# A two-layer decoder trunk: one job list for gate and down projections, and where the block sums are made

## The chip, the cores and the metric

The kernel runs on one core of one Trainium2 chip. The metric is the device time of one execution in microseconds (us); of several runs the median is given. A profile of one execution, taken by the hardware profiler, stands beside the times. The engines are called as the profile calls them: PE (TensorE, with PEld for its weight loads), DVE (VectorE), ACT (ScalarE), POOL (GpSimd) and SP (SyncE, which issues loads).

## The reference

One sequence of 512 tokens, 1024 wide, in float32, goes through two layers. The first mixes tokens with a gated short convolution, the second with sliding-window attention (16 heads, 4 key/value heads, window 128, rotary positions, an attention sink). Each layer ends with a SwiGLU feed-forward network of inner width 2816.

```python
def swiglu(h, w_gate_up, w_down):
    g, u = jnp.split(h @ w_gate_up, 2, axis=-1)
    return (jax.nn.silu(g) * u) @ w_down

for l in range(DEPTH):                       # DEPTH = 2
    if l < N_A:                              # layer 0
        mix = short_conv_mixer(rmsnorm(h, a_pre_norm[l]), a_w_in[l], a_conv_w[l], a_w_out[l])
        h = h + rmsnorm(mix, a_post_norm[l])
    else:                                    # layer 1; K and V from the h after layer 0
        ...
        attn = sliding_window_sink_attention(q, k_sh, v_sh, b_sinks[j]) @ b_w_o[j]
        h = h + rmsnorm(attn, b_post_norm[j])
    ff = swiglu(rmsnorm(h, ffn_pre_norm[l]), ffn_w_gate_up[l], ffn_w_down[l])
    h = h + rmsnorm(ff, ffn_post_norm[l])
```

## The kernel before

**Products.** Every matrix product in float32 is made as three products in a faster float32 format (`mm3`, L171). Each weight block of 128 x 1024 numbers (512 KB) is first split: ACT copies it to the high part (`whi`, L167) and DVE subtracts that from the block to get the low part (`wlo`, L168). `split_weights` (L154) does both on a block that `fetch` (L136) has loaded into a raw buffer with a DMA on SP's queue (L141). There are five raw buffers (`N_RAW`) and five pairs of split buffers (`N_W`). A raw buffer comes free, and the next load can start, when the DVE split of its block is done.

**Stages.** Convolution mixer (0 to 139 us of the profiled execution), its output projection and norms (to 185), feed-forward network (FFN) of layer 0 (to 552), K/V and attention (to 696), its output projection (to 720), FFN of layer 1 (to 1080) and the last writes.

**The FFN** (`ffn`, L685). The inner width of 2816 is cut into 22 tiles of 128, f = 0 to 21. The tiles f = 0 to 3 are projected plainly. The other 18 form nine pairs, called q0 to q8 here. A pair's gate and up projections are made by `gate_seven` (L729), a scheme that gets a product of 2 x 2 blocks from seven block products in place of eight, in the order p = 1, 2, 6, 5, 7, 3, 4. Each of the seven is one weight block and 24 matmuls of 256 columns, so a pair has 168. Three of the seven weight blocks are stored blocks (`w_gb`); four are sums of such blocks.

**The sums of gate blocks** (`Sums`, L396) are made in HBM by DMAs that POOL issues (L408): four copies, two additions, one and one more addition, eight DMAs of 512 KB for each pair, 144 in all. `sum_on` (L433) takes one step of each pair in work. They are called in the convolution stage and after the pairs of both FFNs, and the sums of layer 1 are made from layer 0's FFN on. A finished sum is loaded by SP as any other block (`raw<-hsum`).

**The down projection** is made in four rounds over the tiles, `ROUNDS = [(0, 6), (6, 10), (10, 14), (14, 22)]`. Rounds 0 to 2 are called D0, D1 and D2 here; `seven` (L791) does them by the same scheme, with 126, 84 and 84 matmuls of 512 columns. It loads the four blocks, makes four differences of them on DVE in the raw buffers (L820), and splits with three jobs of lead (`SEVEN_LEAD`, L824 on ACT and L825 on DVE). Its products go into `mix` through DVE (L861). The last round is made directly by `first_half` (L546) and `second_half` (L597), with 192 matmuls.

**Order.** For a layer it is f0 to f3, q0, D0, q1, q2, D1, q3, q4, D2, q5, q6, q7, q8, last round. Each of D0 to D2 stands right behind the pair that makes the last of its activations. `pair_sums` (L708) turns a finished pair into the activation blocks of the down projection: small sums and splits on DVE and ACT, all at once behind the pair. In the gate pairs the order of instructions on an engine is left to a scheduler; in `project_first`, `first_half` and `second_half` it is written out by hand (`manual_schedule`).

**Attention.** POOL does part of the rotary step for most query tiles (L975, L976) and the low part of the split (L982, `rlo`), which the score matmuls (L1034) read. Norms use POOL for a power (L271, L293). The letters R and H in the table of steps `ORDER` stand for the rotary step and its split.

Of the kernel before, what the change touches and what calls it, by code (L numbers as in the profile page):

```python
# [10 lines left out]
F32 = mybir.dt.float32  # L11
F32R = mybir.dt.float32r
# [4 lines left out]
P = 128  # L17
D = 1024
# [6 lines left out]
PLAIN = 4  # L25
WARM = 8
LEAD = 2
SEVEN_LEAD = 3
# [10 lines left out]
N_SLOT, N_WIDE, N_RAW, N_W = 43, 14, 5, 5  # L39
# [17 lines left out]
def yoco_kernel(  # L57
# [337 lines left out]

    class Sums:  # L396

        def __init__(self, l, q):  # L400
            self.a = [w_gb[l, q, b] for b in range(4)]
            self.s = [hbm.tile([P, D], F32, name=name("hsum")) for _ in range(4)]
            self.steps = [self.first, self.second, self.third, self.fourth]

        def move(self, dst, src, behind, **kw):
            dst, src = (a.rearrange("(a b) c -> a (b c)", b=2) for a in (dst, src))
            made = tc.keep_in_program_order(
                nc.gpsimd.dma_start(dst, src, max_dma_last_dim=8 * D, **kw))  # L408
            if behind is not None:
                tc.add_manual_dep(made.ins, behind.ins.name, mybir.DependencyInfo(  # L410
                    mybir.DependencyClass.Sync, mybir.DependencyReason.DATA), reason="pace")

        def first(self, behind):
            a11, a12, a21, a22 = self.a
            for s, a in zip(self.s, (a21, a11, a11, a12)):
                self.move(s, a, behind)

        def second(self, behind):
            a11, a12, a21, a22 = self.a
            self.move(self.s[0], a22, behind, accum_op=ALU.add)  # L420
            self.move(self.s[1], a21, behind, accum_op=ALU.add)

        def third(self, behind):
            self.move(self.s[2], self.s[0], behind, accum_op=ALU.add)

        def fourth(self, behind):
            self.move(self.s[3], self.s[2], behind, accum_op=ALU.add)

    sums_of = {(l, q): Sums(l, q) for l in range(2) for q in range((NF - PLAIN) // 2)}
    to_sum = [sums_of[k] for k in sorted(sums_of)]  # L430
    summing = []

    def sum_on(behind=None, more=True):  # L433

        if more and to_sum:
            summing.append(to_sum.pop(0))
        for x in summing:
            x.steps.pop(0)(behind)
        summing[:] = [x for x in summing if x.steps]
# [74 lines left out]
    for f in range(KT):  # L514
# [27 lines left out]
        if 1 <= f < KT - 1:  # L542
            sum_on(more=f % 2)


    def first_half(load, x, n, take, ws1=None):  # L546

        ws = [load(0, j) for j in range(n // 2)]
        raws = [fetch(load(1, j, True)) for j in range(min(2, n // 2))]
        ws1 = []  # L550

        def more():
            if len(ws1) < n // 2:
                ws1.append(split_weights(None, raws.pop(0), True))
                j = len(ws1) + len(raws)
                if j < n // 2:
                    raws.append(fetch(load(1, j, True)))

        with tc.manual_schedule(engines=ALL):
            pss = [bank("pmix") for _ in range(2)]  # L560
            for t in range(2):
                unit(pss[t], t, ws, x, range(n - 2), n)
                more()
# [107 lines left out]
    def load_out(half, j, raw=False):  # L671
        src = w_out[half, j]
        return src if raw else split_weights(src)
# [4 lines left out]

    ws1 = first_half(load_out, ys, KT, take_out)
    ahead = Ahead(first_weights(0))  # L680
# [4 lines left out]
    def ffn(l, before, ahead, gain, gpres, following):  # L685
# [5 lines left out]
        def gate_pair(pg, pu):  # L691
# [6 lines left out]
            self_paced.append(nc.scalar.activation(gr, pg, AF.Silu))  # L698
# [5 lines left out]
            pair_sums(gr)  # L704

        self_paced = []

        def pair_sums(gr):  # L708
# [7 lines left out]
            nc.scalar.activation(h, a11, AF.Copy)  # L716
            nc.vector.tensor_tensor(out=lo, in0=a11, in1=h.bitcast(F32), op=ALU.subtract)
            for o, x, y, op in ((s1, a21, a22, ALU.add), (s2, s1, a11, ALU.subtract),
                                (s3, a11, a21, ALU.subtract), (s4, a12, s2, ALU.subtract)):
                nc.vector.tensor_tensor(out=o, in0=x, in1=y, op=op)  # L720
            t = [(e[:, :256], e[:, 256:])]
            for src in (*sums, gr[:, S:]):
                h, lo = slot("ahi", F32R), slot("alo", F32R)
                nc.scalar.activation(h, src, AF.Copy)
                nc.vector.tensor_tensor(out=lo, in0=src, in1=h.bitcast(F32), op=ALU.subtract)
                t.append((h, lo))
            acts.append(t)

        def gate_seven(q, factors, out):  # L729
# [3 lines left out]
            a, s = sums_of[l, q].a, sums_of[l, q].s  # L733
            srcs = {1: a[0], 2: a[1], 4: a[3], 5: s[0], 6: s[2], 7: s[1], 3: s[3]}
            chain = {1: "X", 6: "X", 7: "X", 4: "X", 5: "Z", 3: "Z", 2: "Y"}
            pools = {"X": ps_mm, "Y": ps_pt, "Z": ps_sc}
            banks = {}
            gr = wide("gr")
            kept = [slot("st") for _ in range(2)]

            def take(p, e):
                x, y, z = (banks[c][e][:, :256] if c in banks else None for c in "XYZ")
                g0, g1 = (gr[:, c : c + 256] for c in (e * S, e * S + 256))
# [9 lines left out]
                elif p == 3:  # L753
                    nc.vector.tensor_tensor(out=g1, in0=z, in1=s, op=ALU.add)  # L754
                    both = gr[:, e * S : (e + 1) * S]
                    self_paced.append(nc.scalar.activation(both, both, AF.Silu))  # L756
# [5 lines left out]
            for p in (1, 2, 6, 5, 7, 3, 4):  # L762
                whi, wlo = split_weights(srcs[p])
                c = chain[p]
                opened = c not in banks
                if opened:
                    banks[c] = [bank("g" + c.lower(), pools[c]) for _ in range(2)]
                for e in range(2):
                    for k in range(4):
                        kk = slice(e * S + k * P, e * S + (k + 1) * P)  # L770
                        mm3(banks[c][e][:, :256], whi[:, kk], wlo[:, kk], *factors[p][k],
                            opened and k == 0, k == 3 and p in (2, 3, 4), skip_group_check=True)
                    take(p, e)
            out(gr)

        def pair_acts(gr):
            for c in (0, S):
# [4 lines left out]
                acts.append((hi, lo))  # L782
# [8 lines left out]
        def seven(kps, acts, first):  # L791
# [3 lines left out]
            raw = {}  # L795
            for b in range(4):
                for c, ks in enumerate(cs):
                    if len(ks) > 1:
                        raw[b, c] = fetch(w_dn[l, kps[ks[0]] : kps[ks[-1]] + 1, b])
                    else:  # L800
                        raw[b, c] = slot("raw")
                        nc.sync.dma_start(raw[b, c], w_dn[l, kps[ks[0]], b])

            factor = {1: (0, None), 5: (0, 1), 6: (0, 2), 3: (2, None), 7: (1, 2), 2: (3, None),
                      4: (0, 3)}
            jobs = [(p, c) for p in (1, 5) for c in range(len(cs))]
            jobs.sort(key=lambda j: j[1])
            jobs += [(p, c) for p in (6, 3, 7, 2, 4) for c in range(len(cs))]
            ready, banks, left_of = {}, {}, {p: len(cs) for p in factor}
# [5 lines left out]
            def prepare(p, c):  # L815
                b, other = factor[p]
                n = S * len(cs[c])
                w = raw[b, c][:, :n]
                if other is not None:
                    nc.vector.tensor_tensor(out=w, in0=raw[other, c][:, :n], in1=w,  # L820
                                            op=ALU.subtract)
                hi = wsp.tile([P, D], F32R, tag="whi", name=name("whi"))
                lo = wsp.tile([P, D], F32R, tag="wlo", name=name("wlo"))
                nc.scalar.activation(hi[:, :n], w, AF.Copy)  # L824
                nc.vector.tensor_tensor(out=lo[:, :n], in0=w, in1=hi[:, :n].bitcast(F32),  # L825
                                        op=ALU.subtract)
                ready[p, c] = hi, lo

            for j in range(min(SEVEN_LEAD, len(jobs))):
                prepare(*jobs[j])  # L830
            for j, (p, c) in enumerate(jobs):
                if j + SEVEN_LEAD < len(jobs):
                    prepare(*jobs[j + SEVEN_LEAD])
                bs = chain[p]
                if bs not in banks:
                    banks[bs] = [bank("p" + bs.lower(), pools[bs]) for _ in range(2)]
                    opened = True
                else:
                    opened = False
                hi, lo = ready.pop((p, c))  # L840
                left_of[p] -= 1
                for n, k in enumerate(cs[c]):
                    kk = slice(n * S, (n + 1) * S)
                    for r in range(2):
# [4 lines left out]
                if left_of[p]:  # L849
                    continue  # L850
# [34 lines left out]
        for i in (0, 2):  # L885
            gate_pair(*pss[i : i + 2])
# [484 lines left out]
```

## Time and profile before

| | before |
|---|---|
| median of 3 runs | 1086.6 us (1084.23 to 1087.57) |
| the profiled execution | 1089.31 us |
| its span in the profile | 1087.5 us |
| mean granted clock of TensorE | 0.984 |
| busy share of DVE, ACT, POOL | 70%, 51%, 16% |
| moved by DMA | 218.87 MB, mean 201 GB/s |

The page gives the busy time of each engine and the granted clock in 40 slices of the span. A row of the chain of waits has a start, a length and what took it. A row of the timeline has a start, a length, the engine, the line, the operation, its tiles, and in brackets the idle time before it with what ended it. Rows of DMA issues give the count, the size of one and the median time from issue to landing. Matmuls overlap, so that the pace of a stage is read from a window and not from the length of one.

### The profile page before, as it was taken

Reading aid. Unit: us, or ns where it says so; the run is one execution under the profiler, and the core shown is the slowest. Engines: PE = TensorE matmul, PEld = TensorE weight load, DVE = VectorE, ACT = ScalarE, POOL = GpSimd, SP = SyncE. Lnnn points to the kernel's source line nnn. Section 1 sums busy time; section 2 is a strip of 40 time slices with the busy share of each in tenths; the row PEclk is TensorE's granted clock in tenths of the full one; section 3 lists DMA queues with packets and bytes.
Section 4 is the critical chain, followed back from the end, with each engine's and each line's share of the span. In section 5 each row is a group of like instructions: output and inputs, shape, how many; then the busy total and the mean of one; then the engine's idle time right before and its main releaser. Section 6 shows DMA issues by size and latency. Waiting matters only on the chain.

```text
span 1087.5 us, 17067 instructions
## 1 busy us (share of the span) xinstructions
PE 1049.0 (96%) x6556; PEld 940.4 (86%) x6556; DVE 766.5 (70%) x1294; ACT 552.8 (51%) x1000; POOL 172.2 (16%) x227
## 2 busy tenths in 40 slices
PE   9999999999998988999999999999999989989997
PEld 7888888998997977999798888898979879789986
DVE  5765555779677776664678998778786866956654
ACT  6322235845552534553475776677466444445531
POOL 0332201012021110121021541020211101200001
PEclk9999999999999899999999999999999999989999
DMA  9577753287779779899712123325797797878621
GB/s 334 176 209 235 215 191 118 78 270 196 250 219 291 243 219 317 297 309 308 255 44 75 40 79 98 108 107 139 232 275 206 229 332 253 228 249 247 204 99 78
DMA packets 58482, 218.87 MB, mean 201 GB/s; under 512 B 7200, under 2 KB 8096, under 8 KB 49184
## 3 DMA queue, kind: packets, MB, share of 16 engines
q1 hardware_dynamic: 46304, 141.62, 36.8%
q0 software_dynamic: 11520, 75.51, 26.9%
q8 instruction: 51, 0.84, 0.3%
q10 hardware_dynamic: 576, 0.66, 0.2%
q14 instruction: 31, 0.25, 0.1%
HBM read 211.46 MB, written 81.79 MB: 270 GB/s over the span
## 4 chain that ended last, share of the span: by engine, by line
PE 67%; DVE 13%; DMA 13%; ACT 4%; issue 3%; POOL 0%; POOLq 0%; DVEq 0%; SPq 0%; ACTq 0%
DMA raw<-in_w_dn_dram 7%; DMA raw<-hsum 5%; PE gx L172 4%; PE gx L173 4%; PE gx L174 4%; PE pmix L172 3%; PE pmix L173 3%; PE pmix L174 3%; PE pgu L172 3%; PE pgu L173 3%; PE pgu L174 3%; DVE wlo L825 3%; PE gz L172 2%; PE gz L173 2%; PE gz L174 2%
## 5 line engine op out<-in xcount | busy, mean ns | idle before, releaser
L168 DVE TENSOR_TENSOR wlo<-raw,whi 128x1024 fp32r<-128x1024 f32 x168 | 215.0, 1282 | 116.2 <-ACT whi L167 116.1
L167 ACT ACTIVATE whi<-raw 128x1024 fp32r<-128x1024 f32 x168 | 176.9, 1056 | 199.1 <-PE gx L173 44.2
L172 PE MATMUL gx<-xt,whi 128*128 128x256 f32 x432 | 126.5, 293 | 17.6 <-ACT st L746 17.1
L173 PE MATMUL gx<-xt,whi 128*128 128x256 f32 x432 | 125.6, 291 | 0.0
L174 PE MATMUL gx<-xt,wlo 128*128 128x256 f32 x432 | 125.6, 291 | 0.0
L172 PEld LDWEIGHTS gx<-xt,whi 128*128 128x128 f32 x432 | 86.4, 200 | 18.7 <-ACT st L746 17.9
L408 POOL DMA_DIRECT2D hsum<-hsum x36 | 28.6, 854 | 435.4 <-ACT gr L756 265.5
L173 PEld LDWEIGHTS gx<-xt,whi 128*128 128x128 f32 x432 | 86.5, 200 | 0.0
L174 PEld LDWEIGHTS gx<-xt,wlo 128*128 128x128 f32 x432 | 86.5, 200 | 0.0
L408 POOL DMA_DIRECT2D hsum<-in_w_gb_dram x108 | 71.8, 1051 | 71.5 <-ACT gr L756 39.4
L824 ACT ACTIVATE whi<-raw 128x1024 fp32r<-128x1024 f32 (+1 forms) x56 | 52.0, 949 | 57.7 <-DVE raw L820 44.8
L825 DVE TENSOR_TENSOR wlo<-raw,whi 128x1024 fp32r<-128x1024 f32 (+1 forms) x56 | 60.2, 1087 | 18.7 <-ACT whi L824 18.6
L172 PE MATMUL pgu<-xlo,whi 128*128 128x256 f32 (+1 forms) x192 | 61.6, 321 | 0.0
L173 PE MATMUL pgu<-xhi,whi 128*128 128x256 f32 (+1 forms) x192 | 61.1, 318 | 0.0
L174 PE MATMUL pgu<-xhi,wlo 128*128 128x256 f32 (+1 forms) x192 | 61.1, 318 | 0.0
L172 PE MATMUL pmix<-wlo,ahi 128*128 128x512 f32 (+1 forms) x136 | 52.3, 385 | 1.9 <-DVE wlo L162 1.9
L173 PE MATMUL pmix<-whi,ahi 128*128 128x512 f32 (+1 forms) x136 | 51.9, 382 | 0.0
L174 PE MATMUL pmix<-whi,alo 128*128 128x512 f32 (+1 forms) x136 | 51.7, 380 | 0.0
L756 ACT ACTIVATE gr<-gr 128x512 f32<-128x512 f32 x36 | 22.5, 625 | 46.7 <-DVE gr L754 46.5
L820 DVE TENSOR_TENSOR raw<-raw,raw 128x1024 f32<-128x1024 f32 (+1 forms) x32 | 34.8, 1088 | 11.4 <-DMA raw<-in_w_dn_dram 10.9
L172 PE MATMUL gz<-xt,whi 128*128 128x256 f32 x144 | 41.1, 286 | 0.0
L173 PE MATMUL gz<-xt,whi 128*128 128x256 f32 x144 | 41.0, 285 | 0.0
(279 smaller groups left out, 3167.3 us busy)
## 6 DMA issues: line engine op xcount, KB each, us to landing
hsum<-in_w_gb_dram POOLq DMA_DIRECT2D x108, 512.0 KB, 11.7
raw<-hsum SPq DMA_DIRECT2D x72, 512.0 KB, 4.7
raw<-in_w_gb_dram SPq DMA_DIRECT2D x54, 512.0 KB, 7.2
raw<-in_w_dn_dram SPq DMA_DIRECT2D x40, 512.0 KB, 9.0
hsum<-hsum POOLq DMA_DIRECT2D x36, 512.0 KB, 6.5
raw<-in_w_in_dram SPq DMA_DIRECT2D x21, 512.0 KB, 7.2
raw<-in_w_gu_dram SPq DMA_DIRECT2D x16, 512.0 KB, 3.6
raw<-in_w_out_dram SPq DMA_DIRECT2D x8, 512.0 KB, 5.9
```

The costliest lines, as they stand in the source:

```text
L167: nc.scalar.activation(hi, raw, AF.Copy)
L168: nc.vector.tensor_tensor(out=lo, in0=raw, in1=hi.bitcast(F32), op=ALU.subtract)
L172: nc.tensor.matmul(out, whi, xlo, start=start, stop=False, **kw)
L173: nc.tensor.matmul(out, whi, xhi, start=False, stop=False, **kw)
L174: nc.tensor.matmul(out, wlo, xhi, start=False, stop=stop, **kw)
L408: nc.gpsimd.dma_start(dst, src, max_dma_last_dim=8 * D, **kw))
L756: self_paced.append(nc.scalar.activation(both, both, AF.Silu))
L820: nc.vector.tensor_tensor(out=w, in0=raw[other, c][:, :n], in1=w, op=ALU.subtract)
L824: nc.scalar.activation(hi[:, :n], w, AF.Copy)
L825: nc.vector.tensor_tensor(out=lo[:, :n], in0=w, in1=hi[:, :n].bitcast(F32), op=ALU.subtract)
```

## The change

**One list.** Gate products, D0 to D2 and the four first-half weight blocks of the last round become `Job`s in one list, run by `in_line` in an order written out by hand. Before job j + 3 is reached it is prepared (`LINE_LEAD`): its block is split by ACT and DVE while job j's products are issued. Raw blocks are fetched in list order. There are seven raw buffers (`N_RAW`) in place of five and four split pairs (`N_W`) in place of five.

**Late down projection.** The order becomes f2, f3, q0, q1, D0, q2, q3, D1, q4, q5, D2, q6, q7, q8, last round: each of D0 to D2 stands one gate pair later. The activation work of a finished pair comes in six parts, one behind each following job, apart from the jobs that are marked `alone`. D0's 14 products of up to two blocks become 11 jobs, as some half-width blocks share a job.

**Sums.** The four differences of D0 to D2 are now made in HBM too, and DVE's subtraction (L820) is gone. Gate pairs q3, q4 and q5 take all four sums from HBM. The other six (`ADDED`) take two from HBM; the blocks for p = 6 and p = 3 are made by `Job.add` on DVE, in place, from blocks that were loaded for other products, so that such a pair loads five blocks. POOL still issues 144 DMAs. `BEGIN` says at which step each set of sums begins: in the convolution stage and in attention without pacing, in attention between the rotary steps, and in the FFN a few behind each job. The sums of layer 1 begin in attention.

**Smaller ones.** Silu of both halves of a pair comes after p = 3. `first_half` takes ready splits and keeps up to three raw blocks loaded. The sign of one half of `mix` is changed, with a scale where it is begun and a subtraction where it is added to. The host lays out the blocks of `w_dn` differently.

```diff
+ADDED = (0, 1, 2, 6, 7, 8)
+BEGIN = {
+    "c0": "g00", "c2": "g01", "c4": "d00", "c6": "g02", "o0": "g03", "o1": "d01", "0f1": "g04",
+    "0f3": "g05", "0p0": "d02", "0p1": "g06", "0s0": "g07", "0p2": "g08",
+    "a0": "g10", "a2": "g11", "a3": "d10", "a5": "g12", "a6": "g13", "a8": "d11", "1f0": "g14",
+    "1f2": "g15", "1p0": "d12", "1p1": "g16", "1s0": "g17", "1p2": "g18",
+}
-SEVEN_LEAD = 3
+LINE_LEAD = 3
-N_SLOT, N_WIDE, N_RAW, N_W = 43, 14, 5, 5
+N_SLOT, N_WIDE, N_RAW, N_W = 43, 14, 7, 4
...
+        def add(self):
+            if self.make:
+                raw = self.raws[0].tile
+                nc.vector.tensor_tensor(out=raw, in0=raw, in1=self.raws[1].tile, op=ALU.add)
+
+        def prepare(self):
...
+            self.begun = nc.scalar.activation(hi[:, :n], raw, AF.Copy)
+            nc.vector.tensor_tensor(out=lo[:, :n], in0=raw, in1=hi[:, :n].bitcast(F32),
+                                    op=ALU.subtract)
...
+    def in_line(jobs, late):
...
+        def prepare(j):
+
+            if 0 <= j < len(jobs):
+                jobs[j].prepare()
+            while n[0] < len(raws) and (n[0] < N_RAW or raws[n[0] - N_RAW].last <= j):
+                raws[n[0]].fetch()
+                n[0] += 1
+            if j + 1 < len(jobs):
+                jobs[j + 1].add()
+
+        for j in range(-1, LINE_LEAD):
+            prepare(j)
+        for j, job in enumerate(jobs):
+            if job.run:
+                job.run(job)
+            prepare(j + LINE_LEAD)
+            if j + LINE_LEAD < len(jobs):
+                issue(1 + len(issues) // 6, jobs[j + LINE_LEAD].begun)
+            if late and not job.alone:
+                late.pop(0)()
+            late += job.then() or [] if job.then else []
...
+            raws = {1: [a11], 2: [a12], 5: [s1], 7: [s3], 4: [a22]}
+            if rest:
+                raws[6], raws[3] = ([r] for r in rest)
+            else:
+                raws[6], raws[3] = [a11, s1], [a12, a11]
...
-                if other is not None:
-                    nc.vector.tensor_tensor(out=w, in0=raw[other, c][:, :n], in1=w,
-                                            op=ALU.subtract)
...
+                order = [[(1, 0)], [(5, 0)], [(1, 1), (5, 1)], [(6, 0)], [(3, 0)],
+                         [(6, 1), (3, 1)], [(7, 0)], [(2, 0)], [(7, 1), (2, 1)], [(4, 0)],
+                         [(4, 1)]]
...
+                    if behind_one:
+                        jobs += behind_one.pop()
...
     with tc.manual_schedule(engines=ALL):
+        sum_on("a0")
         for i in range(KT + 2):
...
+                if op in "RH":
+                    issue(len(issues) // 2 if op == "R" else len(issues))
+            sum_on(f"a{i + 1}")
```

More of the change, by code (lines that the diff above doesn't have):

```diff
@@ L393, in one, with __init__, fetch @@
             self.lo()
-    class Sums:
[L400 to L406, printed above, removed]
+    class Raw:
+        def __init__(self, *srcs):
+            self.srcs = srcs
+            self.widths = [s.shape[0] * S if len(s.shape) == 3 else D for s in srcs]
+            self.n = sum(self.widths)
+        def fetch(self):
+            self.tile, c = wraw.tile([P, D], F32, tag="raw", name=name("raw")), 0
+            for src, n in zip(self.srcs, self.widths):
+                dst = self.tile[:, c : c + n]
+                if len(src.shape) == 3:
+                    src, dst = (src.rearrange("k p c -> p k c"),
+                                dst.rearrange("p (k c) -> p k c", c=S))
+                nc.sync.dma_start(dst, src)
+                c += n
@@ new lines, in yoco_kernel, with __init__, step @@
+    class Sums:
+        def __init__(self, blocks, shape, every=True):
+            self.blocks = blocks
+            n = 4 if every else 2
+            self.sums = [hbm.tile(shape, F32, name=name("hsum")) for _ in range(n)]
+            a, b, c, d = blocks
+            ab, ac, *rest = self.sums
+            self.steps = [[(ab, a, None), (ac, a, None)], [(ab, b, ALU.add), (ac, c, ALU.add)]]
+            if every:
+                abc, abcd = rest
+                self.steps[0] += [(abc, c, None), (abcd, d, None)]
+                self.steps += [[(abc, ab, ALU.add)], [(abcd, abc, ALU.add)]]
+        def step(self):
+            issues.extend(self.steps.pop(0))
@@ L409, in move @@
             if behind is not None:
[L410 to L430, printed above, removed]
+                tc.add_manual_dep(
+                    made.ins, behind.ins.name, mybir.DependencyInfo(
+                        mybir.DependencyClass.Sync, mybir.DependencyReason.DATA),
+                    reason="pace")
@@ L829, in seven, with run, products @@
[L829 to L833, printed above, removed]
+            def run(parts):
+                def products(job):
+                    at = 0
+                    for p, c in parts:
+                        product(p, c, *(w[:, at : at + S * len(cs[c])] for w in job.w))
+                        at += S * len(cs[c])
+                return products
@@ new lines, in ffn, with weights, take_last @@
+            n = f1 - f0
+            def weights(half, j):
+                return w_dn[l, half : 4 - half : 3 - 2 * half, f0 // 2 + j]
+            closing = [Job([Raw(weights(0, j))], None) for j in range(n // 2)]
+            in_line(jobs + closing, late)
+        res = Update(mix, gain, gpres, True)
+        res.load()
+        def take_last(t, half, ps):
+            res.take(t, half, ps)
+            res.scale(t, half)
+        ws1 = first_half(weights, acts[-1], n, take_last, [job.w for job in closing])
```

345 lines of the change are left out of this document (198 added, 147 removed), and 4 rows, old and new, of the table BEGIN.

## The prediction

> **What bounds the kernel now.** I read the page first, then the stages of the two feed-forward networks (FFN) in the windows view, then the chain of waits and the timeline where a stage ran below pace.
>
> ```profile
> span 1087.5 us, 17067 instructions
> PE 1049.0 (96%) x6556; PEld 940.4 (86%) x6556; DVE 766.5 (70%) x1294; ACT 552.8 (51%) x1000; POOL 172.2 (16%) x227
> PEclk9999999999999899999999999999999999989999
> ```
>
> TensorE is busy 96% of the span, so what can be won without removing matmuls is its idle time, and the slices in which its clock fell. The change keeps all matmuls. So I compare each stage with the same work at full pace (columns: us of the window; busy us and instructions of PE, PEld, DVE, ACT, POOL; granted clock; DMA share; GB/s). First the pace:
>
> ```profile
> 41.03:138.95 97.92, 97.92 (x434) 81.08 (x432) 62.41 (x69) 22.15 (x24) 30.64 (x35) 1.00 0.69 205
> 231.62:251.77 20.15, 20.15 (x170) 20.15 (x168) 16.80 (x26) 10.52 (x17) 1.29 (x3) 1.00 0.69 252
> ```
>
> The convolution stage: 432 matmuls of 512 columns in 97.92 us, 0.2267 us each. Pair q0 of layer 0 (168 matmuls of 256 columns): 20.15 us without a gap. Now layer 0's D0, q1-q2, D1, q3-q4, D2, q5-q8 and the last down projection, then the same of layer 1 (without its last):
>
> ```profile
> 251.77:281.42 29.65, 29.14 (x129) 23.51 (x128) 25.24 (x36) 18.05 (x26) 4.69 (x8) 1.00 0.99 276
> 281.42:321.73 40.31, 40.31 (x338) 40.31 (x336) 27.87 (x39) 20.89 (x33) 3.58 (x6) 1.00 0.74 237
> 321.73:343.63 21.90, 20.14 (x87) 15.43 (x85) 21.27 (x34) 10.43 (x13) 6.78 (x10) 1.00 0.86 246
> 343.63:392.66 49.03, 43.54 (x337) 43.13 (x336) 29.99 (x43) 20.47 (x32) 3.59 (x6) 0.93 0.81 255
> 392.66:416.13 23.47, 21.28 (x87) 16.79 (x85) 22.11 (x34) 10.96 (x14) 6.78 (x10) 0.93 0.82 239
> 416.13:502.25 86.12, 82.17 (x674) 81.96 (x672) 51.77 (x71) 42.26 (x64) 12.45 (x20) 0.98 0.96 305
> 502.25:548.62 46.37, 44.43 (x188) 35.79 (x187) 28.82 (x44) 21.93 (x38) 7.09 (x9) 0.96 0.82 264
> 766.75:786.91 20.16, 20.16 (x170) 20.15 (x168) 16.81 (x26) 10.52 (x17) 1.29 (x3) 1.00 0.72 256
> 786.91:816.58 29.67, 29.17 (x129) 23.50 (x128) 25.24 (x36) 18.06 (x26) 4.69 (x8) 1.00 0.98 275
> 816.58:856.90 40.32, 40.32 (x337) 40.32 (x336) 27.48 (x39) 20.78 (x33) 3.60 (x6) 1.00 0.75 237
> 856.90:879.20 22.30, 20.14 (x87) 15.44 (x86) 21.67 (x34) 10.53 (x14) 6.80 (x10) 1.00 0.85 247
> 879.20:925.66 46.46, 42.12 (x337) 41.90 (x336) 30.07 (x43) 20.61 (x32) 3.60 (x6) 0.96 0.84 267
> 925.66:949.10 23.44, 21.25 (x87) 16.75 (x86) 22.12 (x34) 11.07 (x14) 6.80 (x10) 0.93 0.84 240
> 949.10:1036.45 87.35, 83.49 (x674) 83.28 (x672) 55.58 (x77) 45.26 (x67) 2.34 (x3) 0.96 0.75 232
> ```
>
> q0 to q2 are at full pace, and every stage behind D1 is not. D1 and D2 (84 matmuls, 19.04 us) take 21.90 to 23.47 us with DVE busy 94 to 97%: VectorE bounds them. The pairs behind them lose to this:
>
> ```profile
> 337.79 1.23 DVE wlo L825
> 339.04 13.95 DMA raw<-hsum
> 353.08 1.06 ACT whi L167
> 354.46 0.58 PE L172 MATMUL gx<-xt,whi 128*128 128x256 f32 x1 [4.92 <-ACT st L746]
> 349.20:353.80 4.60, 0.34 (x3) 0.14 (x2) 0.55 (x1) 0.72 (x1) 0.00 (x0) 1.00 1.00 317
> 353.80:360.60 6.80, 6.13 (x28) 6.14 (x29) 4.16 (x5) 4.04 (x7) 0.00 (x0) 0.50 0.99 362
> ```
>
> The chain: a late split in D1 frees a raw buffer only at 339.04, the next block sum is fetched then, lands 13.95 us later, and TensorE stands still for 4.3 of 4.6 us. Then the clock is halved for 6.8 us. One such entry costs about 4.3 + 3.4 = 7.7 us.
>
> **Gate pairs.** Layer 0 spends 20.15 + 40.31 + 49.03 + 86.12 = 195.61 us in its nine pairs, 14.26 more than 9 x 20.15 = 181.35; layer 1 spends 20.16 + 40.32 + 46.46 + 87.35 = 194.29, 12.94 more. The change makes one list of split jobs with three jobs of lead, seven raw buffers in place of five, fetched in list order, and puts each down projection one pair behind the activations it needs, so that a pair follows whose blocks were requested before. Counted in the list of jobs, a load is issued at least 22 us of TensorE work before its use, and the longest landing of a sum above took 13.95. Value taken: all 27.2 us; bounds: none of it (below, as a rival) and all of it.
>
> The six pairs that add on DVE cost it 12 extra additions in a layer:
>
> ```profile
> L820 DVE TENSOR_TENSOR raw<-raw,raw 128x1024 f32<-128x1024 f32 (+1 forms) x32 | 34.8, 1088 | 11.4 <-DMA raw<-in_w_dn_dram 10.9
> L168 DVE TENSOR_TENSOR wlo<-raw,whi 128x1024 fp32r<-128x1024 f32 x168 | 215.0, 1282 | 116.2 <-ACT whi L167 116.1
> ```
>
> Two of 1.09 us bring a pair's 16.8 us of DVE (q0's window) to 19.0, of 20.15, so the pair stays under TensorE: cost 0. With that cover gone, each us over 20.15 would be lost six times in a layer. The addition is also a new wait: on the in-order DVE it stands for two loads, the block and its sum, and behind it are the splits of the next jobs and the sums that empty the PSUM banks. If the load of the sum is late, all of DVE is late; that price is in the rival on late loads. SP's queue carries less, not more: 5 loads in place of 7 in these pairs, while the loads of the block sums stay 72 (48 for gates, 24 of 512 KB for downs).
>
> **Down projections D1, D2.** They now load four ready differences: the 32 subtractions of L820 go. Of D1's 21.27 us four full ones (4.35) leave 16.9, below its 19.04 of matmuls; the activation splits, now one behind each job, leave it as well. Excess: 21.90 + 23.47 - 38.08 = 7.29 in layer 0, 22.30 + 23.44 - 38.08 = 7.66 in layer 1. I keep 0.3 us in each of the four for short waits: -13.75; bounds 0 and -14.95.
>
> **D0.** 126 matmuls need 28.57; its excess, 1.08 us in layer 0 and 1.10 in layer 1, is short waits of a product for its split, on a DVE that is busy 85%. Its new list of 11 jobs, half-width ones among them, has about three times as many such close places: +1 us in each layer, between -1.08 (they vanish) and +2.2 (three times 1.08 in place of it).
>
> **Last down projection, layer 0.** 186 matmuls need 42.17 of 46.37 us. The 0.96 DMA share ahead of it, when layer 1's sums were made under q5 to q8, is gone, as these sums now begin in attention. I take -3.5 of 4.2; bounds 0 and -4.2.
>
> **Sums on POOL's queue.** The 144 moves stay 144: fewer for gates, 36 for downs.
>
> ```profile
> hsum<-in_w_gb_dram POOLq DMA_DIRECT2D x108, 512.0 KB, 11.7
> q0 software_dynamic: 11520, 75.51, 26.9%
> q1 hardware_dynamic: 46304, 141.62, 36.8%
> 577.00:696.00 119.00, 118.59 (x781) 99.88 (x780) 105.22 (x321) 82.42 (x243) 33.46 (x24) 1.00 0.21 67
> 626.23 1.70 POOL L982 TENSOR_TENSOR rlo<-ra,rhi 128x512 fp32r<-128x512 f32 x1 [1.54 <-ACT rhi L981]
> 632.35 0.39 PE L1034 MATMUL psc<-rlo,rhi 64*128 64x256 f32 x2
> ```
>
> Some of them now stand on POOL's queue between the rope steps of attention, where TensorE is busy 118.59 of 119 us. A POOL DMA instruction costs it 6.78 / 10 = 0.68 us (D1's window), at most four come ahead of a step, 2.7 us, and `rlo` ends at 627.93, 4.4 us before its scores start. So they are hidden; I put +1 us for the chains with less slack, in attention and at the norms; bounds 0 and +8 (1 us in each of eight steps).
>
> [...]
>
> **Sum.** -27.2 - 13.75 - 3.5 + 2 + 1 = -41.45. The profiled execution took 1089.31 us (span 1087.5 and 1.8 around it): 1047.9. The median of the three runs, 1086.6, is 2.7 below that execution, so 1045.
>
> **The rivals.**
> *Loads land late all the same.* In 210 to 340 us sums and loads together now ask more of the DMA engines. A move takes 26.9% x 1087.5 / 144 = 2.03 us of all 16, a load some 36.8% x 1087.5 / 270 = 1.48. About 39 moves and 35 loads by my reading of the new order make 131 us in 131. For: D0's window already shows 0.99. Against: the same arithmetic gives 59 us for 281 to 343, where the shares show 49, so about 0.83 load. If half of the entries stay as late as now, 13.6 us come back: 1059; if all, 1072.
>
> *The clock falls anyway.* Half-rate stretches could have another trigger than the stalls.
>
> ```profile
> 396.00:398.00 2.00, 1.30 (x6) 0.74 (x5) 2.00 (x7) 1.54 (x2) 2.00 (x5) 1.00 0.42 66
> 398.00:402.00 4.00, 4.00 (x12) 3.17 (x11) 4.00 (x8) 2.62 (x4) 2.06 (x5) 0.57 0.95 197
> ```
>
> The dip at 398 followed 0.70 us of idle in 2 us. It costs 0.43 x 4 = 1.7 us. Stage clocks below 1 in seven windows lose 0.07 x 49.03 + 0.07 x 23.47 + 0.02 x 86.12 + 0.04 x 46.37 + 0.04 x 46.46 + 0.07 x 23.44 + 0.04 x 87.35 = 13.9 us; if all of it stays, 1059. Against: q0 to q2, without stalls, had 1.00 in both layers. [...]
>
> *Small POOL delays in attention and norms*, 1 us in each of eight steps: 1052.
>
> *Slower.* One mechanism: POOL's queue is in order, and an accumulating move waits for the landing of the copy before it, with rope steps queued behind. If in attention each waits the 11.7 us of a landing in full, a step is 11.7 - 4.4 = 7.3 us late, eight times 58 us, and 1045 + 58 = 1103. It decides from 41.5 / 8 = 5.2 us of delay in each step, a wait of 9.6. Against: they are issued a step apart, some 12 us, while the DMA share there is 0.21.
>
> *The change moves nothing*, because VectorE's work only shifts: 1087. Against it stand D1's 4.35 us of subtractions.
>
> **How the numbers follow.** Forecast 0.67; loads half late 0.07, all late 0.04; clock 0.05; small delays 0.06; slower 0.07; nothing moves 0.04 (a quarter of it slower). What a measurement can tell from no change is about 0.3%, 3.3 us. Faster: 0.67 + 0.11 + 0.05 + 0.06 = 0.89; same 0.03; slower 0.08. The forecast's own bounds: all excess gone and D0's 2.2 too gives 48.5 less, 1038; with D0 at +4.4, POOL at +8 and 5 us of the gates left, 1045 + 2.4 + 7 + 5 = 1059. The range 1037 to 1064 takes in half-late loads, clock and small delays, and leaves out 0.15 of the others and the forecast's tails.
>
> **What would show it.** Right: pairs at 20.15 us each and clock 1.00 through both FFNs; D1 and D2 near 19.3 with DVE under 90%; layer 0's last stage near 43; attention still 119 us. Wrong: TensorE waiting on ACT `whi` behind a load of `hsum` over 14 us between 210 and 340; rope waits on POOL's `hsum`; D0 over 31 us.

## The result, and the profile after

The changed kernel takes 1042.26 us (median, 1041.23 to 1044.98), the kernel before on the same chip 1085.41: a ratio of 0.9605, 95% interval 0.9577 to 0.9633. On a second chip the two took 1043.79 and 1087.8, ratio 0.9595 (0.957 to 0.962). Forecast were 1045 and faster.

The profiled execution took 1044.98 us. Its page:

```profile
span 1043.2 us, 17017 instructions
PE 1031.6 (99%) x6556; PEld 931.4 (89%) x6556; DVE 761.4 (73%) x1280; ACT 552.5 (53%) x994; POOL 170.6 (16%) x227
PEclk9999999999999999999999999999999999999999
```

DVE and ACT work as long as before. TensorE's busy time is 17.4 us shorter with the same matmuls, for the most part the half-rate clock that has gone (30.7 us of the two FFNs at half rate before, 3.4 now; granted 0.984 over the span before, 0.997 now), and its idle time went from 38.5 to 11.6 us. The windows by stage, columns as before: for layer 0 q0-q1, D0, q2-q3, D1, q4-q5, D2, q6-q8 and the last round, then attention, then D0, D1 and D2 of layer 1.

```profile
230.90:271.21 40.31, 40.31 (x337) 40.30 (x336) 33.62 (x54) 25.01 (x41) 8.21 (x14) 1.00 0.94 274
271.21:303.99 32.78, 30.51 (x128) 24.74 (x127) 21.39 (x29) 15.49 (x21) 3.41 (x5) 0.95 0.94 319
303.99:344.30 40.31, 40.31 (x337) 40.31 (x336) 28.43 (x43) 23.49 (x37) 7.67 (x11) 1.00 0.87 256
344.30:363.37 19.07, 19.07 (x87) 15.78 (x85) 17.14 (x23) 8.50 (x8) 1.60 (x2) 1.00 1.03 359
363.37:403.68 40.31, 40.31 (x337) 40.31 (x336) 30.30 (x50) 23.91 (x38) 0.00 (x0) 1.00 0.55 189
403.68:422.75 19.07, 19.07 (x87) 15.77 (x85) 18.51 (x25) 7.53 (x8) 0.00 (x0) 1.00 0.51 165
422.75:483.22 60.47, 60.47 (x505) 60.47 (x504) 44.38 (x61) 34.39 (x51) 0.00 (x0) 1.00 0.47 149
483.22:525.41 42.19, 42.19 (x188) 34.88 (x187) 27.41 (x40) 19.44 (x35) 3.86 (x5) 1.00 0.56 198
553.51:673.76 120.25, 119.71 (x786) 100.50 (x785) 107.19 (x324) 82.58 (x244) 52.17 (x56) 1.00 0.73 207
784.27:812.86 28.59, 28.59 (x128) 23.67 (x127) 20.55 (x28) 15.28 (x21) 3.43 (x5) 1.00 0.91 300
853.17:872.24 19.07, 19.07 (x86) 15.78 (x85) 17.61 (x23) 7.43 (x7) 1.59 (x2) 1.00 0.99 338
912.55:931.62 19.07, 19.07 (x86) 15.78 (x85) 18.51 (x25) 7.52 (x8) 0.00 (x0) 1.00 0.50 166
```

Every gate pair takes its 20.15 us and every D1 and D2 its 19.07. Stage by stage against before: gate pairs of layer 0 195.61 to 181.40 (-14.21) and of layer 1 194.29 to 181.40 (-12.89), D1 and D2 -7.23 and -7.60, the last round of layer 0 -4.18, D0 of layer 1 -1.08, D0 of layer 0 +3.13. That is -44.06 of the 44.3 us by which the span fell. One stage is worse than before, D0 of layer 0, with DMA share 0.94 and clock 0.95. The timeline there (SP's queue, ACT, DVE, TensorE):

```profile
274.58 2.70 SPq L429 DMA_DIRECT2D raw<-hsum  x2
293.12 1.58 ACT L454 ACTIVATE whi<-raw 128x1024 fp32r<-128x1024 f32 x2 [2.40 <-DMA raw<-hsum]
294.21 1.22 DVE L455 TENSOR_TENSOR wlo<-raw,whi 128x1024 fp32r<-128x1024 f32 x1 [2.20 <-ACT whi L454]
297.42 1.28 DVE L1002 TENSOR_TENSOR mix<-mix,px 128x512 f32<-128x512 f32 x2
298.15 0.50 PE L190 MATMUL px<-wlo,ahi 128*128 128x512 f32 x1 [2.27 <-DVE mix L1002]
```

The first of the last two sums of D0 is asked for at 274.58 and lands at 293.0, some 18 us later. ACT waits 2.40 us for it, and DVE 2.20 us for ACT's split. DVE then makes low parts and small sums of activations without a gap, and only at 297.42 begins the `mix` update that frees a PSUM bank. TensorE stands for 2.27 us, although the split of its next block was done at 295.43. The chain of waits names another load:

```profile
278.73 16.22 DMA raw<-in_w_gb_dram
```

That is the stored block behind the two sums. Its landing is long as well, but DVE makes its low part at 299.81, behind the `mix` update, so it isn't what TensorE waited for.

### The profile page after: what moved, and what is told of

It is laid out like the page before. It is cut to its first block, busy times and chain, and to the rows that moved or that the text cites. A ratio compares the mean times of both kernels' runs of the same rounds, so it can differ in the third digit from the quotient of the medians.

```text
span 1043.2 us, 17017 instructions
## 1 busy us (share of the span) xinstructions
PE 1031.6 (99%) x6556; PEld 931.4 (89%) x6556; DVE 761.4 (73%) x1280; ACT 552.5 (53%) x994; POOL 170.6 (16%) x227
## 4 chain that ended last, share of the span: by engine, by line
PE 89%; DVE 4%; DMA 3%; issue 1%; ACT 1%; POOLq 0%; POOL 0%; DVEq 0%; SPq 0%; ACTq 0%
PE gx L192 6%; PE gx L191 6%; PE gx L190 6%; PE pmix L191 5%; PE pmix L192 5%; PE pmix L190 5%; PE gz L192 3%; PE gz L191 3%; PE gz L190 3%; PE pgu L190 3%; PE pgu L191 3%; PE pgu L192 3%; PE px L190 2%; PE px L191 2%; PE px L192 2%; PE pcub L594 2%
## 5 line engine op out<-in xcount | busy, mean ns | idle before, releaser
L455 DVE TENSOR_TENSOR wlo<-raw,whi 128x1024 fp32r<-128x1024 f32 (+1 forms) x188 | 227.7, 1214 | 94.4 <-ACT whi L454 94.4
L454 ACT ACTIVATE whi<-raw 128x1024 fp32r<-128x1024 f32 (+1 forms) x188 | 194.6, 1049 | 82.7 <-DVE raw L445 26.6
L521 POOL DMA_DIRECT2D hsum<-in_w_gb_dram x84 | 55.9, 717 | 120.5 <-ACT whi L454 81.0
L872 ACT ACTIVATE st<-gx 128x256 f32<-128x256 f32 x72 | 27.5, 381 | 84.2 <-PE gx L192 84.2
L289 POOL TENSOR_TENSOR ur<-uv,mhalf 128x1 f32<-128x1 f32 x15 | 11.6, 774 | 358.3 <-DVE uv L285 358.3
L185 ACT ACTIVATE whi<-raw 128x1024 fp32r<-128x1024 f32 x30 | 31.8, 1058 | 65.3 <-PE pb L191 26.3
L186 DVE TENSOR_TENSOR wlo<-raw,whi 128x1024 fp32r<-128x1024 f32 x30 | 49.7, 1665 | 2.9 <-ACT whi L185 2.9
L521 POOL DMA_DIRECT2D hsum<-hsum x24 | 19.2, 825 | 153.2 <-ACT whi L454 87.8
L180 DVE TENSOR_TENSOR wlo<-raw,whi 128x512 fp32r<-128x512 f32 x50 | 33.8, 722 | 12.9 <-ACT whi L179 9.6
L190 PE MATMUL gz<-xlo,whi 128*128 128x256 f32 x144 | 40.8, 283 | 0.0
## 6 DMA issues: line engine op xcount, KB each, us to landing
hsum<-in_w_dn_dram POOLq DMA_DIRECT2D x12, 768.0 KB, 10.8
```

What stands on the lines that cost most here:

```text
L180: nc.vector.tensor_tensor(out=lo[:, c], in0=raw[:, c], in1=hi[:, c].bitcast(F32), op=ALU.subtract)
L185: nc.scalar.activation(hi, raw, AF.Copy)
L186: nc.vector.tensor_tensor(out=lo, in0=raw, in1=hi.bitcast(F32), op=ALU.subtract)
L190: nc.tensor.matmul(out, whi, xlo, start=start, stop=False, **kw)
L289: nc.gpsimd.tensor_tensor(out=self.r[:, t : t + 1], in0=self.v[:, t : t + 1], in1=mhalf[:, :1], op=ALU.pow)
L454: self.begun = nc.scalar.activation(hi[:, :n], raw, AF.Copy)
```

## The experiments

Each kernel was timed beside runs of the kernel before on its chip (medians 1087.8 to 1088.14); ratios are against those.

**1. The kernel before with other buffer counts, nothing else.**

```diff
-N_SLOT, N_WIDE, N_RAW, N_W = 43, 14, 5, 5
+N_SLOT, N_WIDE, N_RAW, N_W = 43, 14, 7, 4        # b_raw7
+N_SLOT, N_WIDE, N_RAW, N_W = 43, 14, 6, 4        # b_raw6
```

> The kernel before with seven raw buffers and four split pairs in place of five and five, nothing else. Theory of lead and relief together: loads are issued two jobs (about 5 us) earlier, so the 4.3 us stalls at the entries of the pairs behind D1 and D2 shrink, but the 15 us of excess in D1 and D2 stay: 1060 to 1075. Rival, buffers alone suffice: pairs at 20.15 us each, 1055 to 1060. Rival, buffers don't matter because the raw buffer is freed by a late DVE anyway: 1082 or more.

> The kernel before with six raw buffers and four split pairs. If each raw buffer brings a load forward by a job (2.7 us of a 4.3 us stall): stalls of about 1.5 us remain at the entries of the pairs behind D1 and D2, 1056 to 1070. If four split pairs, not the raw buffers, were the cure: 1049 to 1053. If it takes both buffers: over 1075.

Measured: seven and four 1050.53 us, ratio 0.9646 (0.9627 to 0.9664); six and four 1054.81, ratio 0.9696 (0.9667 to 0.9725). The first is faster than any theory had it; the second falls between two of them. They bring 37.6 and 33.0 us of the change's 44 without a job list, without a late down projection and without moving a sum. Windows of the first, for layer 0 from D1 on (D1, q3-q4, D2, q5-q8, last round):

```profile
321.64:342.46 20.82, 19.61 (x87) 15.61 (x85) 20.38 (x31) 9.72 (x11) 6.25 (x10) 1.00 0.98 271
342.46:382.78 40.32, 40.32 (x337) 40.32 (x336) 31.60 (x46) 22.25 (x34) 4.14 (x8) 1.00 0.93 304
382.78:403.60 20.82, 19.61 (x86) 15.62 (x85) 20.38 (x31) 9.71 (x11) 6.27 (x10) 1.00 0.99 279
403.60:484.24 80.64, 80.64 (x674) 80.63 (x673) 54.58 (x76) 44.51 (x66) 13.04 (x22) 1.00 0.98 319
484.24:526.43 42.19, 42.19 (x188) 34.86 (x187) 26.59 (x40) 19.99 (x35) 6.55 (x9) 1.00 0.90 300
```

All pairs are at full pace, and so is the last round, under a DMA share of 0.98 and 0.90. The other down rounds are not, and they keep their subtractions: D1 and D2 take 20.82 us with DVE busy 98%, and D0 takes 30.27, 0.6 us more than in the kernel before. With six raw buffers it looks the same but for D1 and D2 at 21.4 to 22.1 us. Behind D1, the last split of an old raw buffer and the load it frees come earlier; SP's queue of the kernel before and of the one with six:

```profile
332.00 11.28 SPq L141 DMA_DIRECT2D raw<-hsum  x4
```

```profile
328.38 10.91 SPq L141 DMA_DIRECT2D raw<-hsum  x4
```

The group of four loads of sums starts 3.6 us earlier, one buffer's worth. No stall is left at the entry: the remainder of 1.5 us that was expected did not come. ACT still waits there for loads of sums, 1.57 and 2.11 us, and the splits that are ready ahead of TensorE cover it. The number of split pairs fell as well, from five to four; whether one of the two counts alone would do was not tried.

**2. The changed kernel with five raw buffers.** `N_RAW` 5 in place of 7.

> The changed kernel with five raw buffers in place of seven. Theory of lead: a load is then issued about five jobs (14 us of TensorE) before its use, below the 16.2 us a landing took in layer 0 near 280 us and above the medians of 5 to 8 us; it loses where the DMA engines are above 0.9 (230 to 360 and 744 to 870): +5 to +30, 1047 to 1072, with dips of the clock. Rival, the list's order and relief are what counts: within 3 us of 1042.

Measured: 1052.18 us (1051.27 to 1059.89), ratio 0.9677 (0.9638 to 0.9715), as the theory of lead had it. Two windows of layer 0, q0-q1 and q2-q3:

```profile
231.06:273.07 42.01, 40.47 (x338) 40.27 (x336) 30.40 (x48) 21.47 (x36) 7.71 (x13) 1.00 0.95 278
304.62:346.49 41.87, 40.82 (x338) 40.41 (x336) 27.94 (x41) 20.55 (x33) 7.69 (x11) 1.00 0.85 246
```

The loss comes where the DMA share is high (0.85 to 0.97 from q0 to D1 of layer 0): 8.2 us from q0 to D1 of layer 0, and 2.1 in q0-q1 and D1 of layer 1. All other gate pairs and down rounds are at pace, and the profiled execution shows no dip of the clock in either FFN (mean granted clock 0.999). So the rest of the change (the list, the late place and the moved sums together) cures most of the illness without the buffers, as the buffers do without the rest: either brings 36 to 38 us, and both 44. Their shares can't be added.

**3. The changed kernel with D0, D1 and D2 at their old place.** The activation work of the pair ahead is then done at once.

```diff
-                    if behind_one:
-                        jobs += behind_one.pop()
...
+                jobs[-1].now = True
...
-                behind_one.append(down)
+                jobs += down
...
+            while job.now and late:
+                late.pop(0)()
```

> The changed kernel with D0, D1 and D2 right behind the pair that makes the last of their activations, whose activation work is then done at once. Theory that the late place matters: the first product of each of six waits for the chain of ACT and DVE work behind the pair, 2 to 5 us, and a half clock behind it costs 1.7 more: +20 to +40, 1062 to 1082. Rival, lead and relief of DVE did nearly all: +0 to +6, 1042 to 1048.

Measured: 1048.11 us (1046.14 to 1048.21), ratio 0.9618 (0.9595 to 0.964): at the upper end of the rival's range. D1 of layer 0:

```profile
321.41:341.74 20.33, 19.69 (x87) 15.62 (x86) 20.21 (x31) 9.31 (x11) 3.42 (x5) 1.00 1.04 338
```

1.26 us over pace, the same in all four of D1 and D2, and 0.85 in each D0 (29.44 us): 6.7 us in all, of which 4.2 come back because D0 of layer 0 no longer stalls. The granted clock is 1.00 in all of these stages. The late place is worth about 1 us for each round.

**4. The changed kernel with the differences of D1 and D2 made on DVE.** In place, four loads in place of seven; 32 POOL moves fewer.

```diff
+                r12, r11, r22, r21 = (Raw(b) for b in sums.blocks)
+                raws = {1: [r11], 5: [r11, r12], 6: [r11, r22], 3: [r22], 7: [r22, r12],
+                        2: [r21], 4: [r21, r11]}
```

> The changed kernel with the differences of D1 and D2 added up on DVE in place again (four additions in each, four loads in place of seven, 32 moves of POOL fewer over both layers); D0 as it was. If DVE's limit in D1 and D2 was a loss by itself: 17.1 to 18.5 + 4.35 us of DVE against 19.07 of matmuls, +2.4 to +3.8 in each of four, 1052 to 1057. Rival, three jobs of lead and the pairs' own slack (DVE 15.2 of 20.15 us) swallow it, and the DMA engines are relieved: 1038 to 1043.

Measured: 1051.47 us, ratio 0.9655 (0.9638 to 0.9672), just below the first theory's range. D1 and D2 of layer 0:

```profile
338.76:358.91 20.15, 19.68 (x87) 15.62 (x86) 20.02 (x28) 8.58 (x10) 1.60 (x2) 1.00 0.67 163
399.22:420.55 21.33, 19.97 (x86) 15.54 (x85) 21.21 (x30) 8.78 (x11) 0.00 (x0) 1.00 0.32 99
```

DVE is busy 99% of both, with more work (20.02 and 21.21 us) than the 19.07 of matmuls: it does bound them, by 1.1 and 2.3 us in each layer, 6.6 in all, less than that theory's 9.6 or more. The rest of what this kernel lost is at the very end of the program (experiment 7). Its D0 of layer 0 is at 28.59, where the changed kernel took 32.78.

**5. Where the gate sums are made.** `ADDED = ()` gives all four sums of each pair to HBM (192 moves), `ADDED` with all nine pairs takes the most from it (120 moves).

> The changed kernel with all four sums of every gate pair from HBM: 48 moves and 24 loads more, 24 DVE additions fewer. If the DMA engines bound the first half of layer 0's FFN (share 0.94 there): sums come late, +5 to +25, 1047 to 1067, with stalls between 210 and 360 us. If DVE bounds it: 1042 or less.

> The changed kernel with two sums on DVE in all nine pairs: 24 moves and 12 loads fewer, 12 DVE additions more, in pairs where DVE is busy 15.2 of 20.15 us. If only the DMA crowd costs time now, D0 of layer 0 loses some of its 4.2 us of excess: 1038 to 1042. If DVE is near its limit behind D1: over 1044.

Measured: all from HBM 1074.99 us, ratio 0.9881 (0.9856 to 0.9907), some 30 us slower than the change and above the range; two on DVE in all 1045.39 (1045.35 to 1046.86), ratio 0.9618 (0.9589 to 0.9647). With all from HBM, D0 and D1 of layer 0:

```profile
279.90:315.43 35.53, 31.02 (x128) 25.12 (x127) 20.59 (x28) 15.13 (x21) 4.44 (x7) 0.90 1.00 344
355.74:380.28 24.54, 21.02 (x87) 16.84 (x85) 18.17 (x27) 9.93 (x11) 3.66 (x5) 0.93 1.04 333
```

The DMA share is 1.00 and 1.04, and D0 and D1 lose 6.9 and 5.5 us. Its first pair starts 8.7 us later besides, as POOL's list reaches into the norms; the chain of waits there:

```profile
160.34 12.18 DMA hsum<-in_w_gb_dram
...
172.80 2.78 POOL hsum L521 x5
175.58 0.61 POOL ur L289
```

A move lands, five more are issued, and only then comes the power that the norm needs. The same happens at the norm behind attention, where the stretch from the last round of layer 0 to q0 of layer 1 takes 269.05 us against 260.74. With two on DVE in all pairs no stage of either FFN is above pace, D0 of layer 0 at 28.59 among them, and still its ratio is no better than the changed kernel's. The time is what the theory of DVE's limit gave, and the cause is not. Its loss lies behind the last write (experiment 7).

**6. The moves of layer 0 later.**

```diff
-    "0p0": "d02", "0p1": "g06", "0s0": "g07", "0p2": "g08",
+    "0s0": "d02", "0p3": "g06", "0s1": "g07", "0p4": "g08",
```

> The changed kernel with four sets of sums of layer 0 begun later (D2's behind D0, those of q6, q7 and q8 behind q3, D1 and q4), which takes up to 16 moves out of 210 to 305 us. If the 16 us landing that stalled D0 of layer 0 comes from the crowd on the DMA engines: D0 28.6 to 30 in place of 32.8, 1038 to 1040. If not: 1042.

> The changed kernel with the four sets of sums begun later, again. If the crowd on the DMA engines was the cause of D0's stall: 1037.5 to 1040.5, at least 1.5 us below the changed kernel on the same chip; if the earlier 1039.4 was luck of the start: no difference.

> The changed kernel as it is, beside the next run on one chip: 1040.5 to 1043.5, with D0 of layer 0 at 30 to 33 us.

Measured: 1039.39 us, ratio 0.9562 (0.9537 to 0.9587); again, beside the changed kernel on one chip, 1040.86 (1039.54 to 1041.17) against 1043.79 (1041.78 to 1044.06), with ratios to the kernel before of 0.9567 (0.9539 to 0.9595) and 0.9595. All five runs are below all five of the changed kernel, by 2.9 us in the median, but the intervals of the two ratios overlap. The last two times are 0.3 to 0.4 us above their ranges; the difference is as the theory of the crowd had it. D0 of layer 0 in the kernel with later moves, and in the changed kernel's second profile:

```profile
269.76:298.35 28.59, 28.59 (x128) 23.66 (x127) 20.55 (x28) 15.29 (x21) 0.78 (x1) 1.00 0.67 226
```

```profile
271.66:303.04 31.38, 28.91 (x128) 23.59 (x127) 19.79 (x27) 15.24 (x21) 3.42 (x5) 1.00 0.97 333
```

With one POOL move in place of five under D0 the DMA share is 0.67 and not 0.97, and the stall is gone, in both profiles of this kernel. The count under D0 isn't all of it: in the changed kernel D0 of layer 1 has POOL's five as well, at 0.91, and runs at pace. But under the two pairs ahead POOL has 14 instructions in layer 0 and 11 in layer 1, and 10 in the kernel with later moves. This is the fastest of the kernels that ran.

**7. Moves that nobody reads.** The kernel with two sums on DVE in all pairs, with POOL's 144 moves kept (the sums of q3 to q5 are still made, and not loaded).

> The changed kernel with two sums on DVE in all nine pairs, but the moves of the sums that nobody reads kept, so that POOL issues 144 again in place of 120. If the number of POOL's moves sets how long POOL drains at the end of the program (10.8 us with 120, 2.9 with 144): 2.9 us and 1037.5 to 1042.5; if not: over 10 us and 1043.5 to 1048. D0 of layer 0 shows besides whether moves (back) or loads (fewer) make its stall: 28.6 or 31 to 33.

Measured: 1042.83 us (1041.5 to 1044.3), ratio 0.959 (0.9561 to 0.9619), between the two ranges. D0 of layer 0 is at 32.37 us again, and moves are all that it has more than the kernel with 120, so they make the crowd. And the end is short again. The DMA share in 40 slices of the last 14 us of the span, 0.35 us each, first with 120 moves, then with 144:

```profile
DMA  2999400000000089991000000000000000000000
```

```profile
DMA  0029994000000000007999000000000399960000
```

With 120 moves the last write ends 7.5 us before the program does, with 144 it is 1.4. In the trace the drain instruction behind POOL's last one takes 10.8 us with 120 moves and 2.9 with 144. With 120 it starts at 1031.95 of a span of 1043.6 us, so the program waits for it.

**8. POOL made to wait in attention.** Both steps of a set of sums are issued at once, so that the addition waits for the landing of the copy.

```diff
             sum_on(f"a{i + 1}")
+            for x in summing:
+                x.step()
+            summing[:] = [x for x in summing if x.steps]
```

> The changed kernel with two steps of a set of sums issued at once in attention, so that POOL waits for a copy to land with the rope steps behind it. If the cover of 4.4 us at the rope steps is what hides POOL's list: a landing of 8 to 9 us costs 4 us in each of six to eight steps, +20 to +35, 1062 to 1077. If landings in attention are 5 us or POOL is idle then anyway: 1042 to 1046.

Measured: 1057.71 us (1055.32 to 1060.52), ratio 0.9728 (0.9696 to 0.976), below the range of the first and far above the second. The waits of TensorE, and POOL's timeline (the last move, then the first power of the norm behind attention):

```profile
PE pmix L190 <- DVE mixo L253: 9.4, 1, 9.4
697.85 0.78 POOL L521 DMA_DIRECT2D hsum<-hsum  x1 [7.29 <-DMA hsum<-hsum]
698.37 0.84 POOL L289 TENSOR_TENSOR ur<-uv,mhalf 128x1 f32<-128x1 f32 x1
```

The rope steps lose only 2.8 us together (attention 123.09 us against 120.25). The list grows late, though, and the norm's power, which stands behind it, holds up TensorE for 9.4 us at one place, with a clock at half rate for 10.2 us behind it (mean granted clock 0.992, against 0.997 in the changed kernel). In the changed kernel the list ends with 4.66 us to spare:

```profile
677.18 0.77 POOL L521 DMA_DIRECT2D hsum<-in_w_dn_dram  x1 [1.14 <-DMA hsum<-in_w_dn_dram]
682.61 0.94 POOL L289 TENSOR_TENSOR ur<-uv,mhalf 128x1 f32<-128x1 f32 x1 [4.66 <-DVE uv L285]
```

## Why the prediction was right, and where its reasons were not

The forecast by sum was -41.45 us against the profiled execution, and -44.33 came.

**Gate pairs.** -27.2 forecast, -27.1 measured. The chain that was read (a split frees a raw buffer late, the load lands 14 us later, TensorE stands, the clock halves) is borne out by the buffers alone removing all of it. But the prediction put list, buffers and late place together as the cure; one more raw buffer (with one split pair fewer) is enough for the stalls.

**D1 and D2.** -13.75 forecast, -14.83 measured. "VectorE bounds them" holds where DVE keeps the work (experiments 1 and 4, DVE at 98 to 99%), but it was not the whole price: with the subtractions still in place, longer lead alone brings D1 and D2 of layer 0 from 45.37 to 41.64 us, half of the 7.23. The term was put down to one cause and had two. The sign was misread besides: "DVE under 90%" did not come, as DVE is busy 90 to 97% of D1 and D2 in the changed kernel, and they are at pace all the same. In these runs it counts whether DVE's work is longer than the 19.07 us of matmuls: 20.38 us in experiment 1, 17.14 to 18.51 in the changed kernel.

**D0.** +2 forecast in all, +2.05 measured, and by another cause. The close places of the list of 11 jobs cost nothing: D0 of layer 1 runs at 28.59. D0 of layer 0 lost 3.13 because a sum landed late under POOL's moves, which stood in the prediction as a rival (the DMA engines full between 210 and 340 us) and came true at one place. Experiments 6 and 7 show that the moves make it. That the total fits is luck. The lead of 22 us that the prediction counted was there: the sum is asked for at 274.58, and TensorE could have begun with it at 295.88. But the landing took 18 of these 21 us, not 13.95, and the work on DVE behind it took more than the rest. So two of the prediction's own signs of being wrong came, a load of a sum of over 14 us and D0 over 31 us.

**Last round of layer 0.** -3.5 forecast, -4.18 measured, and the reason given, that layer 1's sums are gone from the stages before it, fell: in experiment 1 they are made there as before, under a share of 0.98, and the round takes 42.19 us all the same. The step that failed is the 0.96 of DMA share "ahead of it" as the cause: with seven raw buffers the loads landed in time behind a share of 0.98.

**POOL in attention.** +1 forecast, +0.57 measured (119.68 us before the change, 120.25 after it). Even that need not be POOL's doing. The kernel before and the same with seven raw buffers, in attention:

```profile
576.71:696.39 119.68, 119.27 (x787) 100.52 (x785) 105.51 (x321) 82.42 (x243) 33.46 (x24) 1.00 0.21 67
```

```profile
554.54:674.80 120.26, 119.69 (x787) 100.50 (x786) 107.30 (x324) 82.63 (x244) 33.49 (x24) 1.00 0.22 71
```

The second takes as long as the changed kernel, though its POOL moves nothing there; both have more raw buffers and fewer split pairs, and which of the two does it was not tried. The slower rival's mechanism exists, as experiment 8 shows, but its place is the norm behind attention and not the rope steps.

**The clock.** The forecast that the half-rate stretches go with the stalls held: 0.997 over the span. The rival that they stay fell. Its price was mis-added (the seven terms make 15.6 us and not 13.9, so 1061), and the dip at 398 that seemed to lack a stall had one: TensorE was idle for 1.61 of the 3.41 us before it (last section).

**A count.** The down rounds take 48 of POOL's 144 moves, six sets of eight; the prediction's 36 are those that read stored blocks. The forecast doesn't use it.

## What to carry to other kernels

When a stage loses time to loads that land late, ask first when they are requested: here one more landing buffer (with one split pair fewer) did most of what a reordered program does, and the two cures didn't add up. A high share of busy time was no stall by itself here: the last round of layer 0 was at pace behind a DMA share of 0.98 (experiment 1), and D2 of the changed kernel with DVE busy 97%. Moves in HBM cost time where a landing took 18 of the 21 us of lead of its load, and there it was enough to move them to a quieter stretch. Where the chain of waits names a load, check in the timeline that the block which waited is that load's. On an engine that issues such moves, look for the slack of what comes behind the last of them, not only between them: for POOL behind attention it was 4.66 us in the changed kernel, and without it TensorE stood for 9.4 us (experiment 8).

## What the runs showed of the hardware

The end of the program differs between kernels with different counts of POOL moves, and not in order of their number. From the last write to the end of the span it is 1.4 to 1.8 us with 144 moves (the kernel before, the changed one in both profiles, the two of experiment 1, later moves in both profiles, experiment 7), 6.7 with 112 (experiment 4), 7.5 with 120 and 3.5 with 192 (experiment 5). The drain instruction behind POOL's last one takes 2.92 us in the kernel before and in the changed one, both with 144 moves, and 10.8 with 120. Between the kernel with 120 and the padded one of experiment 7 nothing differs but 24 moves whose results nobody reads, so between these two the moves decide it. Why it is so was not tried.

Not each stall halves the clock. In the trace's record of the granted clock, the FFNs of the kernel before have seven stretches at half rate, five of 3.41 us and two of 6.83. Each begins a whole number of 3.41 us behind the one before it (the first three at 353.83, 398.20 and 425.50 us, 13 and 8 times 3.41 apart). The FFNs of the changed kernel have one, of 3.41 us. Windows of that length, in the changed kernel, in its second profile and in the kernel before:

```profile
296.15:299.56 3.41, 1.41 (x6) 1.18 (x7) 3.41 (x8) 2.10 (x3) 0.00 (x0) 1.00 1.03 417
299.56:302.98 3.42, 3.42 (x10) 2.67 (x9) 3.42 (x5) 0.00 (x0) 0.00 (x0) 0.50 0.48 193
```

```profile
293.57:296.98 3.41, 2.76 (x13) 1.95 (x11) 2.09 (x4) 2.71 (x4) 0.00 (x0) 1.00 1.02 417
296.98:300.39 3.41, 1.59 (x7) 1.32 (x8) 3.41 (x7) 2.03 (x3) 0.00 (x0) 1.00 1.03 417
300.39:303.80 3.41, 3.41 (x20) 2.93 (x19) 3.41 (x5) 1.16 (x2) 0.00 (x0) 1.00 0.32 127
```

```profile
394.79:398.20 3.41, 1.80 (x7) 1.19 (x8) 3.35 (x8) 2.83 (x6) 2.56 (x5) 1.00 0.25 38
398.20:401.61 3.41, 3.41 (x10) 2.67 (x9) 3.41 (x6) 2.54 (x4) 1.86 (x4) 0.50 1.10 226
```

In D0 of the changed kernel the stall of 2.27 us leaves 2.00 us idle in one window, and the next is at half rate. In the second profile the stall of 2.47 us lies in two windows, with 0.65 and 1.82 us idle, and the one behind them is at full rate. In the kernel before, the seven windows ahead of a half-rate stretch have 1.61 to 3.41 us of idle TensorE, and of the other windows of its FFNs, laid out in the same way, none at full rate has more than 1.36. So 1.61 us of idle time was followed by half rate in one run, and 1.82 was not in another. The ends of matmuls are modelled, so these idle times are rough. What sets the clock was not tried.
